# The sample group's HGRN state step moved from the projection into the attention stage, in eight pieces; the page table loaded by one transfer and spread by TensorE

## The chip, the core and the metric

One core of one Trainium2 chip runs the whole program. TensorE (PE) multiplies, VectorE (DVE), ScalarE (ACT) and GpSimd (POOL) do elementwise work, SyncE (SP) issues most transfers and ACT some. Each engine takes its instructions strictly in the order of its own list. The metric is the device time of one execution in microseconds (us).

## The reference, cut to what matters

One decoder layer for two groups of tokens that share weights: a prompt of 1024 tokens and a sample group of 8 sequences with one token each. Half of the heads are sparse attention (compressed, selected and window branches), half are HGRN2, a gated linear recurrence. The projection, in short:

```
z = split(rmsnorm(x, g_pre) @ w_in)      # q_a, k/v of three branches, gates, z_a, q_b, f_b, i_b, z_b
f = lb + (1 - lb) * sigmoid(f_b);  k = (1 - lb) * sigmoid(-f_b);  q = silu(q_b);  v = i_b
```

The prompt runs the recurrence in chunks. For the sample group one step of it is left, and this is what the change moves. For each of 8 sequences and 4 heads, with a state S of 128 x 128 (key by value):

```
S_new = f[:, None] * S + k[:, None] * v[None, :]      # an output, hgrn_state_sample
o     = q @ S_new                                     # then rmsnorm, times silu(z_b)
```

The page table (8 sequences x 8 pages, int32) names the rows of the paged caches that the sample group's attention gathers.

## The kernel before, in words

The program has three stages. **Projection** (`project`): `feat` and `tok` multiply the 1032 normalized tokens with `w_in`; weights and tokens are each split into a high and a low part, so that every product is three fp32r matmuls (`w_hi`, `w_lo`, `xhi`, `xlo`; all matmuls go through the helper at L42, all splits through L50 and L51). `load_w` loads eight tiles `w_raw` per call (three buffers), ACT makes `w_hi` (L238), DVE makes `w_lo` (L239). Between the products stand the prompt's HGRN heads (`hgrn_a`, `hgrn_b`), whose DVE steps `AT` (L490 to L552) sit between PE's `ph` products, and whose last step normalizes `O` on POOL (L608) before PE transposes it (L612). **Attention** (`attention`): units of 128 queries and one key head; each block has two `ph` products, an exponential on ACT (`P`, L955), a mask on POOL (L958 to L962) and four `pb` products. Between the blocks stand the score maxima for the unit after the next: a PE product into `pa` (three banks) that DVE reduces (L909, L916, L918) to `Mp` (L923). Every second block also issues a step of the side work: `sample_attention`, with cache rows gathered into `sg` and turned by PE, then `finish_setup`. **Finish**: output and gate products.

A scheduler with its own timing model sets the order of the instructions on every engine, from the order and priority in the code and from the buffers; an engine's list then runs in order.

`hgrn_sample` (L422 to L467) is a generator that `project` steps through, between the HGRN heads 2 and 3. For each of the four heads it loads the states of all eight sequences (`S`, L437) and v broadcast to 128 partitions (`vb`, L439), 512 KB each. DVE multiplies `vb` by k (L441), POOL multiplies `S` by f (L442), DVE adds (L443), SP stores the new state (L444), ACT and DVE split it into `S0h` and `S0l`, and PE multiplies both parts with a padded q (`qp`), 16 matmuls, whose sums DVE adds to `so` (L452 to L455). Buffers: two for `S` and two for `vb`, shared with tiles of the prompt's heads (tags "S", "O", "F").

`page_index` (L645 to L658) loads the page table by eight transfers of 16 x 8 single elements (L651), so that 16 partitions each hold a sequence's row, and adds a lane number.

Of the kernel before, what the change touches and what calls it, by code (L numbers as in the profile page):

```python
# [20 lines left out]
NB = 8  # L21
# [6 lines left out]
class Kernel:  # L28
# [148 lines left out]
    def load_x(self, ctx):  # L177
# [6 lines left out]
        for i in range(9):  # L184
# [39 lines left out]
    def load_w(self, src, *parts):  # L224

        nc = self.nc
        out = []
        width = sum(p[1] for p in parts)
        for k in range(8):
            raw = self.wpool.tile([128, 512], F32, name="w_raw", bufs=3)[:, :width]  # L230
            o = 0
            for c0, n in parts:
                dma = nc.sync.dma_start(raw[:, o:o + n], src[k * 128:(k + 1) * 128, c0:c0 + n])
                o += n
            hi = self.wpool.tile([128, 512], F32R, name="w_hi", bufs=9)[:, :width]
# [44 lines left out]
    def project(self, ctx):  # L280
        nc, a = self.nc, self.a
# [5 lines left out]
        hp = self.hp = self.pool(hctx, "hg", bufs=2)  # L287
# [15 lines left out]
        K, Q, F = {}, {}, {}  # L303
# [30 lines left out]
        st = [self.hgrn_a(h, Q[h], K[h], F[h]) for h in range(2)]  # L334
        self.tok(C_IB, 512, ev_v)
        self.page_index(self.cp)
        smp = self.hgrn_sample()
        next(smp)
        for h in range(2):
            self.hgrn_b(h, *st[h])  # L340
        self.feat((C_FB + 256, 2, ev_f(2)))
        self.feat((C_QB + 256, 2, ev_q(2)))
        go = lambda n: [next(smp, None) for _ in range(n)]
        for h in range(2, 4):
            st = self.hgrn_a(h, Q[h], K[h], F[h])
            go(2 if h == 3 else 0)
            self.hgrn_b(h, *st)
            go(1 if h == 3 else 0)

        def ev_z(dst, scale):  # L350
            def ev(f, ts, p):
# [35 lines left out]
            nc.scalar.dma_start(self.qh_d[f, :, ts], t.bitcast(F32))  # L387
            nc.scalar.dma_start(self.ql_d[f, :, ts], u.bitcast(F32))

        for _ in smp:  # L390
            pass
        self.aux_rows(hp)
        self.tok(C_KC, 256, ev_kv(0))
        self.tok(C_KS, 256, ev_kv(1))
# [24 lines left out]
                nc.sync.dma_start(self.V[:, br, :, h, :64], self.kv_d[1 + br].rearrange("(i p) c -> p i c", p=128)[:, :, 128 + 64 * h:192 + 64 * h])  # L419
        self.feat((C_ZB, 4, ev_z(self.zb_d, self.hgn)), ps=1)  # L420

    def hgrn_sample(self):  # L422

        nc, hp, a = self.nc, self.hp, self.a
        f, k, q = (self.sfkq[:, i] for i in range(3))
        v_d = self.dram.tile([NB, 512], F32, name="v_d")
        self.after(self.pidma, nc.sync.dma_start(v_d, self.vs))
        o = hp.tile([32, 128], F32, name="so", bufs=1)
        for h in range(4):
            yield  # L430
            po = self.ps_t.tile([128, 512], F32, name="pt")[:64, :128]
            qp = hp.tile([128, NB, 64], F32R, name="qp", bufs=1)
            nc.vector.tensor_scalar(qp.rearrange("p (a c) d -> p a (c d)", c=2), self.ones[:, None, :].to_broadcast([128, 4, 128]), 0.0, None, op0=OP.mult)
            qv = qp.rearrange("p b c -> p (b c)")
            self.split(qv[:, h * NB:h * NB + 456:65], qv[:, 32 + h * NB:32 + h * NB + 456:65], q[:, h], nc.vector, nc.vector)
# [3 lines left out]
            nc.sync.dma_start(vb, bass.AP(tensor=v_d.tensor, offset=v_d.offset + h * 128, ap=[[0, 128], [512, NB], [1, 128]]))  # L439
            bc = lambda t: t[:, h, :, None].to_broadcast([128, NB, 128])  # L440
            nc.vector.tensor_tensor(vb, vb, bc(k), op=OP.mult)  # L441
            nc.gpsimd.tensor_tensor(S, S, bc(f), op=OP.mult)  # L442
            nc.vector.tensor_tensor(S, S, vb, op=OP.add)  # L443
            nc.sync.dma_start(a["hgrn_state_sample"][0, :, h].rearrange("b k v -> k b v"), S)  # L444
            hi = hp.tile([128, NB, 128], F32R, name="S0h", tag="F")
            lo = hp.tile([128, NB, 128], F32R, name="S0l", tag="F")
            self.split(hi, lo, S, nc.scalar, nc.vector)
            for b in range(NB):
                self.mm(po, qp[:, b], hi[:, b], b == 0, False)
                self.mm(po[:32], qp[:, b, :32], lo[:, b], False, b == NB - 1)  # L450
            if h:
                nc.vector.tensor_tensor(o, o, po[:32], op=OP.add)  # L452
            else:
                nc.vector.tensor_copy(o, po[:32])
            nc.vector.tensor_tensor(o, o, po[32:], op=OP.add)  # L455
        sq = hp.tile([32, 128], F32, name="ssq", bufs=1)
        ss = hp.tile([128, 1], F32, name="sr", bufs=1)[:32]
        nc.scalar.activation(sq, o, AF.Square, accum_out=ss)
        nc.vector.tensor_scalar(ss, ss, 1.0 / 128, EPS, op0=OP.mult, op1=OP.add)
        r = hp.tile([128, 1], F32, name="srs", bufs=1)[:32]  # L460
        self.rsqrt(hp, r, ss)
        nc.vector.tensor_scalar(o, o, r, None, op0=OP.mult)
        pt = self.ps_t.tile([128, 512], F32, name="pt")[:, :32]
        nc.tensor.transpose(pt, o, self.ident[:32, :32])
        oT = hp.tile([128, 32], F32, name="soT", bufs=1)
        nc.scalar.copy(oT, pt)
        nc.scalar.dma_start(self.oT_d[:, :, T:].rearrange("h v b -> v h b"), oT.rearrange("p (h b) -> p h b", b=NB))  # L467

# [170 lines left out]

    def side_work(self):  # L640
        with ExitStack() as c:
            yield from self.sample_attention(c)
        yield from self.finish_setup(self.fctx)

    def page_index(self, pool):  # L645

        nc = self.nc
        pt = self.a["page_table"]
        raw = pool.tile([128, NB], I32, name="pt_raw", bufs=1)
        for i in range(8):  # L650
            dma = nc.sync.dma_start(raw[16 * i:16 * i + 16], bass.AP(tensor=pt.tensor, offset=pt.offset + i, ap=[[0, 16], [8, NB]]))  # L651
            if i == 0:
                self.pidma = dma
        lane = pool.tile([128, NB], I32, name="pt_lane", bufs=1)
        nc.gpsimd.iota(lane, pattern=[[0, NB]], base=0, channel_multiplier=1)
        nc.vector.tensor_scalar(lane, lane, 15, None, op0=OP.bitwise_and)
        self.pidx = self.cp.tile([128, NB], I32, name="pidx")
        nc.vector.scalar_tensor_tensor(self.pidx, raw, 16.0, lane, op0=OP.mult, op1=OP.add)  # L658

    def gather(self, out, cache, b):  # L660
        rows = cache[0].rearrange("n (r j) a h d -> (n r) (j a h d)", j=8)
# [733 lines left out]
```

## Time and profile before

| | |
|---|---|
| runs | 1085.47, 1088.88, 1092.77 us; median 1088.88 |
| the profiled execution | 1086.7 us, its span 1085.0 us |
| mean granted clock of TensorE | 0.991 |
| PE busy | 1047.7 us, 97% of the span |
| DVE / ACT / POOL busy | 617.8 / 388.4 / 243.9 us |

The projection's last stores are issued at 546.5 us; attention's exponentials run from 548.1 to 846.4 us, with the finish beside their later part and after it. PE is the engine that is nearly always busy, so what counts is where PE waits, and where its granted clock (1.00 is 2.4 GHz, 0.50 is 1.2 GHz) is low. Idle time of another engine counts only where PE, or the end, waits for it.

### The profile page before, as it was taken

How to read it: one execution, taken by the hardware profiler on the slowest of the kernel's cores; microseconds unless marked ns; L12 is line 12 of the kernel's file. 1: busy time of each engine (PE TensorE's matmuls, PEld its weight loads, DVE VectorE, ACT ScalarE, POOL GpSimd, SP SyncE). 2: the span in 40 equal slices, each digit the busy share in tenths (PEclk: the TensorE clock that was granted, in tenths of full speed). 3: DMA queues.
4: the chain of work that ended last, by engine and by line, in shares of the span. 5: the costliest groups of instructions: out<-in, count | busy, mean ns of one | idle time of the engine just before them, and what ended most of it. 6: DMA issues, size and time to landing. Idle time of an engine off the chain costs nothing.

```text
span 1085.0 us, 18918 instructions
## 1 busy us (share of the span) xinstructions
PE 1047.7 (97%) x7021; PEld 933.6 (86%) x7021; DVE 617.8 (57%) x1822; ACT 388.4 (36%) x786; POOL 243.9 (22%) x276
## 2 busy tenths in 40 slices
PE   4999999999899999999989999999999999999998
PEld 3898799999889899999968888888788888778876
DVE  6847565665494634543665656766665686471223
ACT  4622234313132335432234544553554232241112
POOL 0014232331041133002032211121323133131111
PEclk9999999999989999999989999999999999999999
DMA  6212023323464766403568611001831573121110
GB/s 195 79 29 69 11 72 100 117 89 119 131 176 142 214 210 211 148 1 107 129 215 266 154 29 51 20 21 53 227 106 40 161 209 90 41 97 49 49 35 30
DMA packets 118815, 116.44 MB, mean 107 GB/s; under 512 B 18710, under 2 KB 100974, under 8 KB 116420
## 3 DMA queue, kind: packets, MB, share of 16 engines
q1 hardware_dynamic: 97220, 79.46, 25.7%
q10 hardware_dynamic: 19200, 19.01, 5.1%
q0 software_dynamic: 2304, 16.78, 4.5%
q8 instruction: 55, 0.90, 0.4%
q14 instruction: 36, 0.29, 0.1%
HBM read 84.84 MB, written 29.31 MB: 105 GB/s over the span
## 4 chain that ended last, share of the span: by engine, by line
PE 82%; DMA 9%; DVE 4%; issue 2%; ACT 2%; POOL 1%; SPq 0%; ACTq 0%; DVEq 0%; POOLq 0%
PE pa L42 39%; PE pb L42 26%; PE ph L42 9%; PE pt L42 4%; DMA vb<-v_d 2%; DMA w_raw<-w_in 2%; PE ph L717 1%; PE pa L1125 1%; DMA fw_raw<-w_out 1%; DMA fw_raw<-ple_gate 1%; DMA x_in<-x_prompt 1%; DVE fw_lo L51 1%; PE ph L1319 1%; DMA gpre<-g_pre 0%; DMA f_oa<-oa_d 0%
## 5 line engine op out<-in xcount | busy, mean ns | idle before, releaser
L42 PEld LDWEIGHTS pb<-V,P 128*128 128x128 f32 x1056 | 141.8, 191 | 12.1 <-POOL P L960 1.2
L42 PE MATMUL pb<-V,P 128*128 128x128 f32 x1056 | 148.1, 276 | 0.4 <-DVE mx L909 0.4
L42 PE MATMUL pa<-xhi,w_hi 128*128 128x344 f32 x384 | 126.0, 330 | 2.6 <-ACT w_hi L238 1.1
L42 PE MATMUL pa<-xlo,w_hi 128*128 128x344 f32 x384 | 124.5, 326 | 0.0
L42 PE MATMUL pa<-xhi,w_lo 128*128 128x344 f32 x384 | 123.5, 327 | 0.0
L955 ACT ACTIVATE P<-ph 128x512 f32<-128x512 f32 (+4 forms) x148 | 85.6, 595 | 98.6 <-PE ph L42 69.3
L916 DVE CUSTOM_DVE_ANT_0 junk<-pa,mask 128x320 bf16<-128x320 f32 (+5 forms) x150 | 72.9, 497 | 27.8 <-PE pa L42 26.6
L42 PE MATMUL pa<-w_lo,xhi 128*128 128x256 f32 (+2 forms) x256 | 79.5, 314 | 0.0
L42 PE MATMUL pa<-w_hi,xlo 128*128 128x256 f32 (+2 forms) x256 | 79.2, 314 | 0.0
L42 PE MATMUL pa<-w_hi,xhi 128*128 128x256 f32 (+2 forms) x256 | 78.6, 316 | 0.0
L42 PEld LDWEIGHTS pa<-xhi,w_hi 128*128 128x128 f32 x384 | 73.5, 192 | 4.2 <-ACT w_hi L238 1.7
L238 ACT ACTIVATE w_hi<-w_raw,gpre 128x512 fp32r<-128x512 f32 (+2 forms) x80 | 47.5, 616 | 78.2 <-DMA w_raw<-w_in 43.0
L42 PEld LDWEIGHTS pa<-xlo,w_hi 128*128 128x128 f32 x384 | 73.5, 192 | 0.1
L42 PEld LDWEIGHTS pa<-xhi,w_lo 128*128 128x128 f32 x384 | 73.0, 191 | 0.2
L42 PE MATMUL ph<-QA,KA 128*128 128x512 f32 (+4 forms) x148 | 66.7, 453 | 3.8 <-ACT P L955 2.9
L42 PE MATMUL pa<-KB,QB 65*128 65x320 f32 (+6 forms) x195 | 63.4, 363 | 0.1
L239 DVE SCALAR_TENSOR_TENSOR w_lo<-w_raw,gpre,w_hi 128x512 fp32r<-128x512 f32 (+2 forms) x80 | 50.6, 653 | 21.4 <-ACT w_hi L238 20.7
L42 PE MATMUL pa<-fw_hi,yh 128*128 128x512 f32 (+1 forms) x160 | 61.9, 387 | 0.2 <-ACT fw_hi L50 0.2
L42 PE MATMUL pa<-fw_lo,yh 128*128 128x512 f32 (+1 forms) x160 | 61.6, 385 | 0.0
L42 PE MATMUL pa<-fw_hi,yl 128*128 128x512 f32 (+1 forms) x160 | 61.6, 385 | 0.0
L42 PE MATMUL ph<-QB,KB 68*128 68x512 f32 (+4 forms) x148 | 58.5, 406 | 0.0
L559 POOL TENSOR_TENSOR K<-K,E 128x512 f32<-128x512 f32 x24 | 36.4, 1517 | 94.2 <-PE pb L42 57.2
(457 smaller groups left out, 2411.9 us busy)
## 6 DMA issues: line engine op xcount, KB each, us to landing
w_raw<-w_in SPq DMA_DIRECT2D x32, 256.0 KB
w_raw<-w_in SPq DMA_DIRECT2D x48, 128.0 KB
VS<-sg SPq DMA_DIRECT2D x8, 512.0 KB
sg<-cache_win_kv SPq DMA_DIRECT2D x16, 256.0 KB
fw_raw<-w_out SPq DMA_DIRECT2D x16, 256.0 KB
fw_raw<-ple_gate SPq DMA_DIRECT2D x16, 256.0 KB
f_x<-x_prompt SPq DMA_DIRECT2D x8, 512.0 KB
win_kv_sample<-cache_win_kv SPq DMA_DIRECT2D x8, 511.0 KB
```

Of the source, the lines that this page charges most:

```text
L42: return self.nc.tensor.matmul(out, lhsT, rhs, start=start, stop=stop, skip_group_check=True)
L51: lo_eng.tensor_tensor(lo, src, hi.bitcast(F32), op=OP.subtract)
L238: nc.scalar.activation(hi, raw, AF.Copy, scale=g)
L239: nc.vector.scalar_tensor_tensor(lo, raw, g, hi.bitcast(F32), op0=OP.mult, op1=OP.subtract)
L559: nc.gpsimd.tensor_tensor(Kv[:, :, 0], Kv[:, :, 0], Ev[:, :, 1:2].to_broadcast([128, nb, m]), op=OP.mult)
L717: nc.tensor.transpose(pt[:, i * 128:(i + 1) * 128], src[b0 + j // 2, kv][:, j % 2, 2 * jp:2 * jp + 2].rearrange("p j d -> p (j d)"), self. ...
L916: nc.vector.tensor_tensor_reduce(junk, pm, mk, 1.0, -1e30, op0=OP.add, op1=OP.max, accum_out=o)
L955: nc.scalar.activation(P, ps, AF.Exp, scale=0.125)
L1125: nc.tensor.transpose(pt[:, j * 128:(j + 1) * 128], rows(j), self.ident)
L1319: nc.tensor.transpose(pt[:, c], h[:, k * 128:(k + 1) * 128], self.ident[:n, :n])
```

## The change

The page table comes by one transfer of 8 rows and 8 columns. DVE converts it to float, POOL makes a 0/1 matrix that repeats each row for 16 partitions, and one small matmul spreads it into a PSUM tile, to which DVE adds the lane number. The transfer is ordered behind the last weight transfer of the i_b columns.

The sample group's HGRN step leaves `project`; only the store of v to memory (`v_d`) stays there. `hgrn_sample` now works on half a head at a time (4 sequences, 256 KB per load or store), eight pieces, in a pool of its own with one buffer per tile (`hS`, `hvb`, `hSh`, `hSl`, `qp`), sums in a `pa` bank, and has two yields per piece: after the split, and after the sums. `side_work` steps it from the ninth step of `sample_attention` on, one yield per step. Lines of `attention` and `finish` are 11 higher afterwards.

```diff
@@ load_w
-                dma = nc.sync.dma_start(raw[:, o:o + n], src[k * 128:(k + 1) * 128, c0:c0 + n])
+                dma = self.lastw = nc.sync.dma_start(raw[:, o:o + n], src[k * 128:(k + 1) * 128, c0:c0 + n])
@@ project
         self.page_index(self.cp)
-        smp = self.hgrn_sample()
-        next(smp)
+        self.v_d = self.dram.tile([NB, 512], F32, name="v_d")
+        self.after(nc.sync.dma_start(self.v_d, self.vs), self.pidma)
...
-        go = lambda n: [next(smp, None) for _ in range(n)]
         for h in range(2, 4):
-            st = self.hgrn_a(h, Q[h], K[h], F[h])
-            go(2 if h == 3 else 0)
-            self.hgrn_b(h, *st)
-            go(1 if h == 3 else 0)
+            self.hgrn_b(h, *self.hgrn_a(h, Q[h], K[h], F[h]))
...
-        for _ in smp:
-            pass
         self.aux_rows(hp)
@@ hgrn_sample
+        hp = self.pool(ctx, "hsamp", side="right")
         for h in range(4):
-            yield
-            po = self.ps_t.tile([128, 512], F32, name="pt")[:64, :128]
-            S = hp.tile([128, NB, 128], F32, name="S0", tag="S")
-            vb = hp.tile([128, NB, 128], F32, name="vb", tag="O")
+            for b0 in (0, 4):
+                S = hp.tile([128, 4, 128], F32, name="hS")
+                nc.sync.dma_start(S, a["state_hgrn"][0, b0:b0 + 4, h].rearrange("b k v -> k b v"))
+                vb = hp.tile([128, 4, 128], F32, name="hvb")
+                nc.sync.dma_start(vb, bass.AP(tensor=self.v_d.tensor, offset=self.v_d.offset + b0 * 512 + h * 128, ap=[[0, 128], [512, 4], [1, 128]]))
+                nc.vector.tensor_tensor(vb, vb, bc(k), op=OP.mult)
+                nc.gpsimd.tensor_tensor(S, S, bc(f), op=OP.mult)
+                nc.vector.tensor_tensor(S, S, vb, op=OP.add)
+                nc.sync.dma_start(a["hgrn_state_sample"][0, b0:b0 + 4, h].rearrange("b k v -> k b v"), S)
+                self.split(hi, lo, S, nc.scalar, nc.vector)
+                yield
+                po = self.ps_a.tile([128, 512], F32, name="pa")[:64, :128]
+                for b in range(4):
+                    self.mm(po, qp[:, b], hi[:, b], b == 0, False)
+                    self.mm(po[:32], qp[:, b, :32], lo[:, b], False, b == 3)
...
+                yield
@@ side_work
-            yield from self.sample_attention(c)
+            state = self.hgrn_sample(c)
+            for j, _ in enumerate(self.sample_attention(c)):
+                if j >= 8:
+                    next(state, None)
+                yield
+            for _ in state:
+                yield
@@ page_index
-        for i in range(8):
-            dma = nc.sync.dma_start(raw[16 * i:16 * i + 16], bass.AP(tensor=pt.tensor, offset=pt.offset + i, ap=[[0, 16], [8, NB]]))
+        self.pidma = nc.sync.dma_start(raw, bass.AP(tensor=pt.tensor, offset=pt.offset, ap=[[1, 8], [8, NB]]))
+        self.after(self.pidma, self.lastw)
+        nc.vector.tensor_copy(num, raw)
...
+        self.mm(p, sel, num, True, True)
```

How it moves instructions is shown at three places. The first is SP's list at the start of the projection (L651 and L652 are the page table, L233 weight tiles, L244 copies of a cache):

```order
-L233 DMA w_raw<-w_in 128x256 x6
-L651 DMA pt_raw<-page_table 16x8x1 x7
-L233 DMA w_raw<-w_in 128x256 x10
+L233 DMA w_raw<-w_in 128x256 x16
 L233 DMA w_raw<-w_in 128x512 x8
 L244 DMA win_kv_sample<-cache_win_kv 16x8176 x2
+L652 DMA pt_raw<-page_table 8x8x1
```

The seven transfers that stood between the third and the fourth pair of weight transfers are gone; the single one stands 26 transfers later.

The second is DVE's list in HGRN heads 2 and 3 of the prompt. Before (L441 and L443 are the sample step; AT are the prompt heads' steps for which PE's next `ph` products wait):

```order
L51 TENSOR_TENSOR PRl<-PR,PRh 128x512
L369 COPY z_s<-pa 128x256
L441 TENSOR_TENSOR vb<-vb,sfkq 128x1024
L520 COPY_PREDICATED AT<-lm_496,ph 128x512
L51 TENSOR_TENSOR PQl<-PQ,PQh 128x1024
L490 COPY_PREDICATED AT<-lm_495,pt 128x512
L369 COPY z_s<-pa 128x256 x2
L441 TENSOR_TENSOR vb<-vb,sfkq 128x1024
L513 COPY_PREDICATED AT<-lm_498,ph 128x256x2
```

The same place in the changed program (lines 4 lower here):

```order
L51 TENSOR_TENSOR PRl<-PR,PRh 128x512
L365 COPY z_s<-pa 128x256
L516 COPY_PREDICATED AT<-lm_496,ph 128x512
L51 TENSOR_TENSOR PQl<-PQ,PQh 128x1024
L486 COPY_PREDICATED AT<-lm_495,pt 128x512
L365 COPY z_s<-pa 128x256
L509 COPY_PREDICATED AT<-lm_498,ph 128x256x2
```

The two multiplications of `vb` no longer stand ahead of the steps L520 (now L516) and L513 (now L509).

The third is the attention stage of the changed program. SP's list there (hS and hvb are the pieces' loads, L437 their stores, QA and QB the queries of a later unit):

```order
L437 DMA hgrn_state_sample<-hS 128x4x128
L432 DMA hvb<-v_d 128x4x128
L895 DMA QA<-qh_d 64x4x128
L895 DMA QB_5305<-qh_d 64x4x128
L895 DMA QA<-ql_d 64x4x128
L430 DMA hS<-state_hgrn 128x4x128
L432 DMA hvb<-v_d 128x4x128
L437 DMA hgrn_state_sample<-hS 128x4x128
L430 DMA hS<-state_hgrn 128x4x128
L1006 DMA oa_d<-og 128x256
L432 DMA hvb<-v_d 128x4x128
```

and DVE's list from one piece's multiplication (L434) over its addition (L436) to the next piece's multiplication (L927 and L929 reduce maxima, PT and KT are splits of the sample attention):

```order
L434 TENSOR_TENSOR hvb<-hvb,sfkq 128x512
L51 TENSOR_TENSOR qp<-sfkq,qp 128x4
L927 ISA junk,mx<-pa,mask 128x384
L927 ISA mx 128x1
L920 ISA junk,mx<-pa,mkc 128x64
L920 ISA mx 128x1
L51 TENSOR_TENSOR PT<-pt,PT 128x64x8
L929 TENSOR_REDUCE mx<-pa 128x1
L436 TENSOR_TENSOR hS<-hS,hvb 128x512
L51 TENSOR_TENSOR KT_6932<-pa,KT_6931 128x512
L929 TENSOR_REDUCE mx<-pa 128x1
L434 TENSOR_TENSOR hvb<-hvb,sfkq 128x512
```

On PE the first matmuls of the eight pieces stand at matmul 3609, 3659, 3707, 3740, 3765, 3831, 3892 and 3921 of its list. Every load of a piece stands behind the store of the one before or behind the addition that reads its buffer, and two rows of DVE lie between an addition and the next multiplication, whose load can start only after that addition.

## Rows read from the trace of the kernel before

**Rows 1.** The page, busy time by engine, then the chain that ended last, by line.

```profile
PE 1047.7 (97%) x7021; PEld 933.6 (86%) x7021; DVE 617.8 (57%) x1822; ACT 388.4 (36%) x786; POOL 243.9 (22%) x276
PE pa L42 39%; PE pb L42 26%; PE ph L42 9%; PE pt L42 4%; DMA vb<-v_d 2%; DMA w_raw<-w_in 2%; PE ph L717 1%; PE pa L1125 1%; DMA fw_raw<-w_out 1%; DMA fw_raw<-ple_gate 1%; DMA x_in<-x_prompt 1%; DVE fw_lo L51 1%; PE ph L1319 1%; DMA gpre<-g_pre 0%; DMA f_oa<-oa_d 0%
```

**Rows 2.** Waits of PE: waiting line, what ended it, us in total, times, longest.

```profile
PE ph L42 <- DVE AT L513: 3.6, 1, 3.6
...
PE ph L42 <- DVE AT L520: 2.9, 1, 2.9
...
PE pt L612 <- POOL O L608: 2.6, 1, 2.6
...
PE pa L42 <- ACT w_hi L238: 1.1, 2, 0.9
```

**Rows 3.** The chain that ended last, 280 to 400 us: start, duration, piece of work.

```profile
282.81 5.47 DMA vb<-v_d
288.37 1.23 DVE vb L441
289.60 1.20 DVE AT L520
...
351.77 7.82 DMA vb<-v_d
359.61 1.24 DVE vb L441
361.05 2.86 POOL O L608
...
381.94 0.96 PE pt L42 x16
```

**Rows 4.** Busy time by stretch: engines' busy us, granted clock (PEclk), DMA share, GB/s.

```profile
290.00:300.00 10.00, 6.22 (x44) 5.86 (x44) 5.02 (x7) 0.38 (x2) 0.00 (x0) 0.99 0.57 162
300.00:306.00 6.00, 5.33 (x24) 5.36 (x25) 4.76 (x6) 1.24 (x2) 5.30 (x3) 0.50 0.68 207
364.00:368.00 4.00, 4.00 (x18) 4.00 (x19) 0.05 (x1) 0.68 (x2) 0.00 (x0) 0.59 0.81 265
```

**Rows 5.** The chain and SP's issues in the first 40 us.

```profile
16.85 3.27 SPq L651 DMA_DIRECT2D pt_raw<-page_table  x7
...
20.64 7.24 DMA w_raw<-w_in
...
29.86 2.26 DMA w_raw<-w_in
```

**Rows 6.** Busy time by stretch again: late projection, and attention.

```profile
300.00:320.00 20.00, 19.33 (x198) 18.70 (x199) 18.71 (x36) 7.11 (x12) 10.05 (x6) 0.83 0.55 161
605.00:656.00 51.00, 51.00 (x350) 45.42 (x349) 34.66 (x126) 26.55 (x48) 11.54 (x16) 1.00 0.26 71
```

**Rows 7.** The sample step's operations by line or tile: ns min/median/max, first and last start.

```profile
L442 POOL TENSOR_TENSOR S<-S,sfkq x4: 1898/1900/2495, 300.1 to 354.4; 128x1024 f32<-128x1024 f32 x4
L443 DVE TENSOR_TENSOR S<-S,vb x4: 1203/1218/2155, 302.1 to 360.9; 128x1024 f32<-128x1024 f32 x4
L51 DVE TENSOR_TENSOR S0l<-S,S0h x4: 1206/1209/1226, 308.4 to 378.2; 128x1024 fp32r<-128x1024 f32 x4
L433 DVE TENSOR_SCALAR qp<-ones x4: 404/411/995, 3.1 to 375.9; 128x512 fp32r<-128x512 f32 x4
L455 DVE TENSOR_TENSOR so<-so,pt x4: 278/280/280, 314.4 to 383.2; 32x128 f32<-32x128 f32 x4
```

**Rows 8.** Timeline of POOL and DVE where two of these operations lie beside another engine's.

```profile
302.59 2.50 POOL L442 TENSOR_TENSOR S<-S,sfkq 128x1024 f32<-128x1024 f32 x1 [0.61 <-DMA S<-state_hgrn]
305.05 1.15 POOL L559 TENSOR_TENSOR K<-K,E 128x512 f32<-128x512 f32 x1
...
302.12 1.21 DVE L443 TENSOR_TENSOR S<-S,vb 128x1024 f32<-128x1024 f32 x1
...
305.12 2.15 DVE L443 TENSOR_TENSOR S<-S,vb 128x1024 f32<-128x1024 f32 x1 [1.14 <-POOL S L442]
```

More of the change, by code (lines that the diff above doesn't have):

```diff
@@ L420, in project, with hgrn_sample @@
         self.feat((C_ZB, 4, ev_z(self.zb_d, self.hgn)), ps=1)
-    def hgrn_sample(self):
-        nc, hp, a = self.nc, self.hp, self.a
+    def hgrn_sample(self, ctx):
+        nc, a = self.nc, self.a
         f, k, q = (self.sfkq[:, i] for i in range(3))
-        v_d = self.dram.tile([NB, 512], F32, name="v_d")
-        self.after(self.pidma, nc.sync.dma_start(v_d, self.vs))
-        o = hp.tile([32, 128], F32, name="so", bufs=1)
+        hp = self.pool(ctx, "hsamp", side="right")
+        o = hp.tile([32, 128], F32, name="so")
@@ L429, in hgrn_sample @@
         for h in range(4):
-            yield
-            po = self.ps_t.tile([128, 512], F32, name="pt")[:64, :128]
[L432 to L435, printed above, removed]
@@ L436, in hgrn_sample @@
-            S = hp.tile([128, NB, 128], F32, name="S0", tag="S")
-            nc.sync.dma_start(S, a["state_hgrn"][0, :, h].rearrange("b k v -> k b v"))
-            vb = hp.tile([128, NB, 128], F32, name="vb", tag="O")
[L439 to L457, printed above, removed]
+            for b0 in (0, 4):
+                qp = hp.tile([128, 4, 64], F32R, name="qp")
+                nc.vector.tensor_scalar(qp.rearrange("p (a c) d -> p a (c d)", c=2), self.ones[:, None, :].to_broadcast([128, 2, 128]), 0.0, None, op0=OP.mult)
+                qv = qp.rearrange("p b c -> p (b c)")
+                c0 = h * NB + b0
+                self.split(qv[:, c0:c0 + 196:65], qv[:, 32 + c0:32 + c0 + 196:65], q[:, h, b0:b0 + 4], nc.vector, nc.vector)
+                S = hp.tile([128, 4, 128], F32, name="hS")
+                nc.sync.dma_start(S, a["state_hgrn"][0, b0:b0 + 4, h].rearrange("b k v -> k b v"))
+                vb = hp.tile([128, 4, 128], F32, name="hvb")
+                nc.sync.dma_start(vb, bass.AP(tensor=self.v_d.tensor, offset=self.v_d.offset + b0 * 512 + h * 128, ap=[[0, 128], [512, 4], [1, 128]]))
+                bc = lambda t: t[:, h, b0:b0 + 4, None].to_broadcast([128, 4, 128])
+                nc.vector.tensor_tensor(vb, vb, bc(k), op=OP.mult)
+                nc.gpsimd.tensor_tensor(S, S, bc(f), op=OP.mult)
+                nc.vector.tensor_tensor(S, S, vb, op=OP.add)
+                nc.sync.dma_start(a["hgrn_state_sample"][0, b0:b0 + 4, h].rearrange("b k v -> k b v"), S)
+                hi = hp.tile([128, 4, 128], F32R, name="hSh")
+                lo = hp.tile([128, 4, 128], F32R, name="hSl")
+                self.split(hi, lo, S, nc.scalar, nc.vector)
[4 more added lines that the diff above has]
+                    self.mm(po[:32], qp[:, b, :32], lo[:, b], False, b == 3)
+                if c0:
+                    nc.vector.tensor_tensor(o, o, po[:32], op=OP.add)
+                else:
+                    nc.vector.tensor_copy(o, po[:32])
+                nc.vector.tensor_tensor(o, o, po[32:], op=OP.add)
+                yield
@@ L458, in hgrn_sample @@
+        sq = hp.tile([32, 128], F32, name="ssq")
+        ss = hp.tile([128, 1], F32, name="sr")[:32]
         nc.scalar.activation(sq, o, AF.Square, accum_out=ss)
         nc.vector.tensor_scalar(ss, ss, 1.0 / 128, EPS, op0=OP.mult, op1=OP.add)
-        r = hp.tile([128, 1], F32, name="srs", bufs=1)[:32]
+        r = hp.tile([128, 1], F32, name="srs")[:32]
         self.rsqrt(hp, r, ss)
         nc.vector.tensor_scalar(o, o, r, None, op0=OP.mult)
-        pt = self.ps_t.tile([128, 512], F32, name="pt")[:, :32]
+        pt = self.ps_a.tile([128, 512], F32, name="pa")[:, :32]
@@ L464, in hgrn_sample @@
         nc.tensor.transpose(pt, o, self.ident[:32, :32])
-        oT = hp.tile([128, 32], F32, name="soT", bufs=1)
+        oT = hp.tile([128, 32], F32, name="soT")
         nc.scalar.copy(oT, pt)
@@ L648, in page_index @@
         pt = self.a["page_table"]
-        raw = pool.tile([128, NB], I32, name="pt_raw", bufs=1)
-        for i in range(8):
-            dma = nc.sync.dma_start(raw[16 * i:16 * i + 16], bass.AP(tensor=pt.tensor, offset=pt.offset + i, ap=[[0, 16], [8, NB]]))
-            if i == 0:
-                self.pidma = dma
+        raw = pool.tile([8, NB], I32, name="pt_raw", bufs=1)
+        self.pidma = nc.sync.dma_start(raw, bass.AP(tensor=pt.tensor, offset=pt.offset, ap=[[1, 8], [8, NB]]))
+        self.after(self.pidma, self.lastw)
+        num = pool.tile([8, NB], F32, name="pt_num", bufs=1)
+        nc.vector.tensor_copy(num, raw)
+        sel = self.zpool.tile([128, 688], F32, name="z_s", bufs=2)[:8, :128]
+        nc.gpsimd.memset(sel, 1.0)
+        nc.gpsimd.affine_select(sel, sel, pattern=[[1, 128]], compare_op=OP.is_ge, fill=0.0, base=0, channel_multiplier=-16)
+        nc.gpsimd.affine_select(sel, sel, pattern=[[-1, 128]], compare_op=OP.is_ge, fill=0.0, base=15, channel_multiplier=16)
         lane = pool.tile([128, NB], I32, name="pt_lane", bufs=1)
@@ L656, in page_index @@
         nc.vector.tensor_scalar(lane, lane, 15, None, op0=OP.bitwise_and)
+        lf = pool.tile([128, NB], F32, name="pt_lf", bufs=1)
+        nc.vector.tensor_copy(lf, lane)
+        p = self.ps_t.tile([128, 512], F32, name="pt")[:, :NB]
+        self.mm(p, sel, num, True, True)
         self.pidx = self.cp.tile([128, NB], I32, name="pidx")
-        nc.vector.scalar_tensor_tensor(self.pidx, raw, 16.0, lane, op0=OP.mult, op1=OP.add)
+        nc.vector.scalar_tensor_tensor(self.pidx, p, 16.0, lf, op0=OP.mult, op1=OP.add)
     def gather(self, out, cache, b):
```

## The prediction

> **What bounds the kernel now.** I read four views, from the whole to the place. The page first: PE is busy 97% of the span, and in the chain that ended last nearly every large share is PE's own work; the one transfer of the sample step in it, the load of `vb`, has 2% [rows 1]. So only PE's waits and its clock can give much back. Then PE's waits: three of the longest stand in the projection, 3.6, 2.9 and 2.6 us, on the DVE steps L513 and L520 and on POOL's L608; a wait of 0.9 on `w_hi` belongs to the head [rows 2]. Then the chain through them, read in order of time: the load of `vb` takes 5.47 us, DVE's multiplication of it follows at once (L441, 1.23), and only behind that comes the step L520 that PE waits for. The same at 351.77: 7.82 us of loading, 1.24 on DVE, then POOL's normalization of the prompt's `O`, then PE [rows 3]. DVE stood in its list at a multiplication whose operand was still in flight, with the prompt's work queued behind it. Last the clock by stretch: in 300 to 306 it is 0.50, and in 364 to 368 it is 0.59, each behind one of these waits; in 290 to 300, where two of the waits lie, it is still 0.99 [rows 4].
>
> **What the change takes away.**
> - The three waits. The two multiplications ahead of L520 and L513 are gone from DVE's list, and so is the one ahead of the last head's normalization. Each load that held DVE, 5.47 to 7.82 us, is longer than the PE wait it caused, so I take all of 3.6 + 2.9 + 2.6 = 9.1 us. What is late next there is the prompt's own chain PE, DVE, PE. If the largest wait stayed for that reason, 5.5 us would be left; that is the low end.
> - The clock. Half of the 6 us at 0.50 is lost time, 3.0 us; at 0.59, 41% of 4 us, 1.6 us; 4.6 us in all [rows 4]. With no wait ahead of them both stretches should run at 2.4 GHz. The stretch from 290 to 300 shows that a wait need not be followed by a slow stretch, so the low end is 0 for a wait that stays.
> - The head. SP spends 3.27 us on seven page-table transfers, then the next `w_raw` is 7.24 us under way, where a later one needs 2.26 [rows 5]. ACT's `w_hi` comes late, but PE has other products queued and loses only the 0.9 us [rows 2]. I take 0.9; the bounds are 0 and the 3.27 us of SP.
> - PE's own work is the same 64 matmuls: 16 take 0.96 us [rows 3], 3.8 us in either place.
>
> The gain is 9.1 + 4.6 + 0.9 = 14.6 us.
>
> **What it adds in attention.** In 605 to 656 us, where pieces 3 to 8 will lie, PE is busy all 51 us with 350 matmuls, 0.146 us each, DVE 34.66 us [rows 6]. Two prices are to be compared.
> - DVE's work. At half the size of before, a piece has three long operations of 0.60 us (half of 1203 and 1206 ns), 0.2 for `qp`, two small splits taken at half of a `so` addition, 0.14 each, and two `so` additions of 0.28 [rows 7]: 2.8 us. Six pieces are 17 us: 51.7 of 51. The densest stretch of the projection has DVE at 18.71 of 20 us, 94% [rows 6]; at that share 51.7 needs 55, so PE is held back by about 4 us, less if the maxima lag without harm.
> - The chain of one piece through its single buffers: load, POOL's multiplication, DVE's addition, store, and only then the next load. A load of 128 KB takes 2.26 us [rows 5], one of 512 KB 5.47 [rows 3]; for 256 KB I take 3.3, on the line between them, and the same for the store, which no row shows. SP's two issues are 0.9 (3.27 / 7 each [rows 5]), POOL 0.95 and DVE 0.60 [rows 7]. Together 3.3 + 3.3 + 0.9 + 0.95 + 0.60 = 9.0 us; with both transfers at 2.26 it is 7.0, at 5.47 13.4. Between the first matmuls of pieces 3 and 8 stand 214 PE matmuls, 31 us at 0.146. Five rounds of 9.0 are 45 us; loads may run about one round ahead of PE, so some 5 us are missing. At 7.0 nothing is missing, at 13.4 27 us.
>
> Both prices point at the same place and partly overlap; I take 6 us of PE waits, with 0 and 15 as ends (15 is 45 less 31, no lead at all). The work waiting behind is known: DVE's reductions of maxima stand right behind the multiplication of `hvb` and the addition, PE's next products into `pa` wait for their banks, and on SP the next unit's queries `QA` and `QB` stand behind a store and a load. For the clock I add one slow stretch at the smaller of the two prices, 1.6 us (0 to 4.6). The first piece's `qp` operations come ahead of the first unit's `Mp`: 0.5 us. The small page-table matmul has the time of one in sixteen of 0.96, 0.06 us; its operand is loaded behind the last weights of the v products, and those products, which PE works off first, cover the transfer, so I cost its wait at nothing. If that cover were gone, PE would wait for one small transfer, 2.3 us.
>
> Transfers of 6 MB move from the projection, with its DMA share of 0.57 in 290 to 300 [rows 4], to a stretch with 0.26 [rows 6]; I take no cost for that.
>
> The Trainium skill, page "DMA: Bandwidth & Descriptors", section "Measured (HBM→SBUF, 128 partitions, SWDGE, issued from GpSimd)", speaks against the pieces: it says to batch transfers to 1 MiB or more for three quarters of the peak rate. By its fixed cost of about 2.0 us and 436 GB/s (section "Anatomy of one DMA — SWDGE (gpsimd) path"), an estimate for a piece is 2.6 us per transfer, a chain of 7.7 us and hardly a wait; the trace agrees that there is a fixed part (1.2 us on the line through 2.26 and 5.47 us), but moves the rest at about 120 GB/s [rows 3, 5].
>
> **The sum.** -14.6 + 6 + 1.6 + 0.5 + 0.1 = -6.4. From the profiled execution's 1086.7 that is 1080.3. It lies 2.2 us under the median of the runs, 1088.88, so on that scale 1082.5.
>
> **The rivals.**
> 1. *The cover holds.* Loads run further ahead than one round or the maxima have room, and PE never waits for a piece. For it: PE 100% busy in that stretch with DVE idle a third of it. Against: single buffers, and only 25 matmuls (3.7 us) between pieces 4 and 5. Price: -14.6 + 0.6 = -14.0, on the runs' scale 1074.9.
> 2. *Slower: the chain of single buffers becomes the bound.* From piece 1 to piece 8 stand 312 matmuls, 45.6 us. Seven rounds of 9.0 without lead are 63, which costs 17.4. Each wait of the size of those in the projection [rows 2] may bring a slow stretch; with two, 4.6 more, and DVE held at `hvb` rows holds the maxima for the rest of a load, 3.3 less the two rows between, about 2 us on some two of the pieces, 4 us. In all -14.6 + 0.6 + 17.4 + 4.6 + 4 = +12: 1098.7, on the runs' scale 1100.9. It decides from a round of 6.5 us (45.6 / 7) up, if the loads get no lead. For it: the order of SP's list, where a load stands behind its own buffer's store. Against: the first two pieces have more room.
> 3. *DVE and POOL hold each other up.* An addition beside POOL's L559 took 2.15 us where 1.21 is usual; a POOL multiplication beside a DVE addition took 2.50 where 1.90 is usual [rows 8]. The late one seems to wait for the other's whole operation. POOL is busy 11.5 of 51 us there [rows 6], 30% with 0.95 more for each of four pieces; 24 new long DVE operations, hit three times in ten, at half of the 0.94 us: 3.4 us more waits. Price: -3.0, on the runs' scale 1085.9. The Trainium skill has this as a rule (page "SBUF — State Buffer", section "Who interferes with whom"): a DVE instruction with two SBUF inputs contends with a GpSimd instruction that reads SBUF, and the second fully waits. The trace agrees, with the 0.94 and 0.60 us above.
> 4. *The projection does not give it back.* The prompt's heads wait on their own PE, DVE, PE chain once `vb` is out of the way. Half of the gain, 7.3, against costs of 8.2: +0.9, 1089.8 on the runs' scale. Against: in the chain the loads are the longest pieces by far [rows 3].
>
> **How the numbers follow.** About 1% (10.9 us) is what the runs can tell from no change, since they spread by 7 us. Chances: my forecast 0.32, rival 1 0.27, rival 2 0.16, rival 3 0.14, rival 4 0.11. Faster than 1078 takes rival 1 and a twentieth from the forecast's better end: 0.32. Slower than 1099.8 takes most of rival 2: 0.13. The rest is 0.55. The forecast's own range is 1077 to 1087; the range for 8 in 10 reaches from rival 1's 1074.9 less the head's upper bound (2.4 more), 1072, to 1098, which cuts the upper part of rival 2 and the tails.
>
> **What would show it.** Right: no wait of PE on L516, L509 or L604 (L608 before) above 1 us, the clock at 1.00 in 285 to 370, the first `w_raw` landings without a 7 us one, and between 600 and 670 PE waits of some 6 us in all that end on DVE's reductions or on `hSl`, with DVE waiting for `hvb`. Rival 1 shows attention without such waits; rival 2 shows DVE or POOL waiting for a load in each piece, several us each, and slow stretches; rival 3 shows long `hvb` or `hS` rows on DVE beside POOL's. My forecast is wrong if the waits in the projection stay under other names, or if SP's list delays the queries of a unit.

## The result and the profile after

The change makes the kernel slower: 1101.97 us (median of 6 runs) against 1086.49 us for the kernel before, measured beside it; ratio 1.0121, 95% interval [1.0095, 1.0147]. The forecast was 1082.5 with a range of 1072 to 1098. The profiled execution of the change spans 1098.4 us.

Busy time by stretch, the kernel before. The stretches are the projection up to the first exponential of attention, attention from the first to the last exponential's start, and the rest; columns: stretch, its length, then PE, PEld, DVE, ACT, POOL busy (instructions), granted clock, DMA share, GB/s.

```profile
0.00:548.10 548.10, 520.91 (x3808) 493.46 (x3808) 318.98 (x774) 188.71 (x410) 116.46 (x129) 0.99 0.39 117
548.10:846.40 298.30, 293.06 (x2104) 255.06 (x2105) 188.48 (x782) 140.18 (x250) 74.87 (x116) 0.98 0.37 106
846.40:1085.00 238.60, 233.68 (x1112) 185.03 (x1110) 110.34 (x268) 59.52 (x127) 52.52 (x33) 1.00 0.28 86
```

The same of the changed kernel:

```profile
0.00:530.50 530.50, 511.42 (x3745) 486.49 (x3745) 299.71 (x734) 185.28 (x404) 106.49 (x128) 1.00 0.35 109
530.50:860.00 329.50, 315.23 (x2169) 270.48 (x2170) 216.10 (x860) 146.72 (x261) 82.80 (x124) 0.94 0.41 115
860.00:1098.40 238.40, 233.90 (x1111) 184.92 (x1109) 104.37 (x263) 59.82 (x127) 52.19 (x33) 1.00 0.27 86
```

The balance is in these six rows. The projection is 17.6 us shorter, the rest is unchanged, attention is 31.2 us longer. In attention PE idles 14.3 us (length less PE busy) where it idled 5.2. The mean clock falls from 0.98 to 0.94: the stretches at 0.50 add up to 10.2 us in the attention of before and to 40.9 us in that of the change, and half of such a stretch is lost, 5.1 and 20.5 us. And 64 matmuls more are done there, 3.8 us by their price of before. These three make 28.3 of the 31.2 us.

The projection's gain is where it was expected. The stretch of [rows 3, 4], the kernel before and then the changed one:

```profile
270.00:310.00 40.00, 33.48 (x230) 31.98 (x229) 23.28 (x32) 8.69 (x19) 7.51 (x5) 0.91 0.53 155
```

```profile
270.00:310.00 40.00, 40.00 (x377) 38.66 (x376) 26.13 (x45) 11.10 (x24) 7.37 (x7) 1.00 0.43 130
```

PE has no wait left there and runs at full clock. Waits of PE in the changed kernel (columns as in [rows 2]; left out is the one of 10.4 us at the program's start, the same before):

```profile
PE pa L42 <- DVE mx L927: 4.0, 2, 3.5
PE ph L42 <- ACT P L966: 3.3, 4, 1.7
PE ph L728 <- DVE cr L721: 2.5, 1, 2.5
PE pa L42 <- DVE sm L1072: 2.3, 1, 2.3
PE pa L42 <- DVE Mp L934: 2.3, 3, 1.4
```

The three waits of [rows 2] on L513, L520 and L608 are gone; L728 is a new one of 2.5 us, later in the projection, with a short stretch at half clock behind it; the others are in attention. That stretch:

```profile
370.00:374.00 4.00, 3.02 (x11) 3.02 (x12) 1.79 (x8) 1.85 (x3) 2.25 (x2) 0.59 0.92 324
```

The largest wait of attention, followed through the timelines of DVE and SP (start, duration, instruction, in brackets the idle time ahead and its end):

```profile
611.03 0.69 DVE L436 TENSOR_TENSOR hS<-hS,hvb 128x512 f32<-128x512 f32 x1 [1.30 <-POOL hS L435]
...
618.12 0.69 DVE L434 TENSOR_TENSOR hvb<-hvb,sfkq 128x512 f32<-128x512 f32 x1 [4.37 <-DMA hvb<-v_d]
...
619.13 0.47 DVE L927 CUSTOM_DVE_ANT_0 junk<-pa,mask 128x320 bf16<-128x320 f32 x1
...
624.22 0.69 DVE L436 TENSOR_TENSOR hS<-hS,hvb 128x512 f32<-128x512 f32 x1 [1.69 <-POOL hS L435]
...
628.88 1.39 DVE L434 TENSOR_TENSOR hvb<-hvb,sfkq 128x512 f32<-128x512 f32 x1
```

```profile
611.75 0.38 SPq L437 DMA_DIRECT2D hgrn_state_sample<-hS  x1
612.18 0.50 SPq L432 DMA_DIRECT2D hvb<-v_d  x1
612.77 0.61 SPq L895 DMA_DIRECT2D QA<-qh_d  x1
```

The load of `hvb` could be issued only after the addition at 611.03, stood behind the store, and took 5.84 us in the chain; DVE stood at L434 for 4.37 us with a reduction of maxima behind it, and PE waited 3.5 us for that. What follows costs more (changed kernel, by stretch):

```profile
615.00:620.00 5.00, 1.51 (x12) 1.28 (x11) 1.88 (x6) 0.22 (x1) 1.26 (x1) 0.99 0.40 93
620.00:627.00 7.00, 4.17 (x26) 3.48 (x25) 5.22 (x29) 1.93 (x3) 1.11 (x2) 0.74 0.20 57
627.00:647.00 20.00, 19.57 (x77) 16.23 (x76) 12.48 (x37) 7.29 (x15) 4.09 (x5) 0.50 0.34 101
647.00:660.00 13.00, 13.00 (x95) 11.80 (x95) 8.61 (x30) 4.88 (x9) 4.01 (x5) 0.99 0.25 72
```

For 20 us PE is busy nearly all the time at half clock and does 77 matmuls; the next 13 us hold 95.

### The profile page after: what moved, and what is told of

Same layout as the page of the kernel before. It is cut to its first block, busy times and chain, and to the rows that moved or that the text cites. A ratio compares the mean times of both kernels' runs of the same rounds, so it can differ in the third digit from the quotient of the medians.

```text
span 1098.4 us, 18967 instructions
## 1 busy us (share of the span) xinstructions
PE 1060.6 (97%) x7023; PEld 941.9 (86%) x7023; DVE 620.2 (56%) x1856; ACT 391.8 (36%) x790; POOL 241.5 (22%) x283
## 4 chain that ended last, share of the span: by engine, by line
PE 83%; DMA 6%; DVE 5%; issue 4%; ACT 2%; POOL 0%; SPq 0%; DVEq 0%; POOLq 0%; ACTq 0%
PE pa L42 39%; PE pb L42 26%; PE ph L42 9%; PE pt L42 3%; DMA fw_raw<-w_out 1%; PE ph L728 1%; PE pa L1136 1%; DMA hS<-state_hgrn 1%; DMA hvb<-v_d 1%; DVE junk L927 1%; DMA fw_raw<-ple_gate 1%; DMA cg<-cache_cmp_kv,pidx 1%; DVE fw_lo L51 1%; PE ph L218 1%; DMA w_raw<-w_in 1%
## 5 line engine op out<-in xcount | busy, mean ns | idle before, releaser
L42 PEld LDWEIGHTS pb<-V,P 128*128 128x128 f32 x1056 | 145.4, 198 | 11.3 <-issue 1.1
L42 PE MATMUL pb<-V,P 128*128 128x128 f32 x1056 | 152.6, 284 | 0.6 <-DVE onrm L1000 0.4
L927 DVE CUSTOM_DVE_ANT_0 junk<-pa,mask 128x320 bf16<-128x320 f32 (+5 forms) x150 | 73.4, 496 | 24.1 <-PE pa L42 22.8
L42 PE MATMUL ph<-QA,KA 128*128 128x512 f32 (+4 forms) x148 | 69.2, 470 | 4.3 <-ACT P L966 3.3
L42 PE MATMUL pa<-KB,QB 65*128 65x320 f32 (+6 forms) x195 | 65.8, 369 | 6.7 <-DVE mx L927 4.0
L239 DVE SCALAR_TENSOR_TENSOR w_lo<-w_raw,gpre,w_hi 128x512 fp32r<-128x512 f32 (+2 forms) x80 | 53.1, 684 | 19.6 <-ACT w_hi L238 17.9
L42 PE MATMUL ph<-QB,KB 68*128 68x512 f32 (+4 forms) x148 | 61.0, 423 | 0.0
```

The costliest lines, as they stand in the source:

```text
L42: return self.nc.tensor.matmul(out, lhsT, rhs, start=start, stop=stop, skip_group_check=True)
L927: nc.vector.tensor_tensor_reduce(junk, pm, mk, 1.0, -1e30, op0=OP.add, op1=OP.max, accum_out=o)
```

## Experiments

Theory 1 was what this timeline suggests: engines stand at loads that go through single buffers. Theory 3 holds the transfers and SP's list responsible. Theory 4 is that the pieces' instructions in the engines' lists, in whatever engine, cost attention its time, with the slow clock behind the small gaps of PE. In all, 14 runs; their attention stretch, from the first to the last exponential, by the same view. The time and the ratio are from all executions of a run, the three columns behind them from its one profiled execution:

| run | us | ratio to the kernel before [95%] | attention, us | PE idle in it | clock in it |
|---|---|---|---|---|---|
| kernel before | | 1 | 298.3 | 5.2 | 0.98 |
| the change | 1101.97 | 1.0121 [1.0095, 1.0147] | 329.5 | 14.3 | 0.94 |
| E1 step left out | 1076.36 | 0.9896 [0.9869, 0.9923] | 304.1 | 7.3 | 0.98 |
| E2 no loads | 1096.44 | 1.0087 [1.0057, 1.0117] | 325.9 | 12.2 | 0.94 |
| E3 transfers, split, products | 1088.40 | 1.0007 [0.9986, 1.0027] | 320.7 | 8.7 | 0.94 |
| E4 page table alone | 1082.21 | 0.9938 [0.9913, 0.9962] | 300.0 | 5.6 | 0.98 |
| E5 two buffers | 1098.60 | 1.0097 [1.0067, 1.0126] | 328.7 | 14.9 | 0.95 |
| E6 loads ahead | 1098.04 | 1.0104 [1.0069, 1.0139] | 329.2 | 13.0 | 0.94 |
| E7 no products | 1099.48 | 1.0121 [1.0062, 1.0180] | 322.1 | 14.5 | 0.94 |
| E8 before z_a | 1122.05 | 1.0315 [1.0260, 1.0370] | 294.5 | 3.5 | 0.98 |
| E9 quarter heads | 1127.47 | 1.0351 [1.0290, 1.0413] | 305.7 | 7.2 | 0.97 |
| E10 transfers alone | 1081.39 | 0.9932 [0.9893, 0.9970] | 309.8 | 7.5 | 0.96 |
| E11 on POOL | 1098.22 | 1.0120 [1.0082, 1.0158] | 325.1 | 14.7 | 0.96 |
| E12 late | 1125.75 | 1.0342 [1.0280, 1.0405] | 355.6 | 28.6 | 0.89 |
| E13 own buffers for v | 1075.40 | 0.9860 [0.9827, 0.9894] | 299.8 | 7.1 | 0.98 |
| E14 the change again | 1103.08 | 1.0117 [1.0075, 1.0158] | 334.4 | 15.9 | 0.93 |

**E1.** 

> The change with the sample group's step left out of attention: one memory-to-memory transfer writes the old states as the output, ones stand for its result; everything else as in the change. Theory 1 (attention loses to the pieces, whatever in them): the projection keeps its gain, attention runs as before the change, 17.6 us under the kernel before, ratio about 0.984 (1069 us). Rival (the projection's gain itself upsets attention, by other arrival times and another order of the list): still above 1085.

```diff
-        for h in range(4):
-            for b0 in (0, 4):
...
+        nc.sync.dma_start(a["hgrn_state_sample"][0], a["state_hgrn"][0])
+        nc.vector.tensor_copy(o, self.ones[:32])
+        yield
```

The one transfer is issued at 16.6 us, far ahead of attention. 1076.36: 12 us faster than before, not 17.6. Attention gets most of its length back (304.1), but 6 us stay lost with no piece in it. The list around it is another one: of attention's 2104 matmuls of before, 1972 stand in the same order. The pieces have the other 25 us. That the order costs the 6 us is not shown, but where it is that of before throughout (E4, E13), attention takes 300.0 and 299.8 us.

**E2.** 

> The change with the pieces' two loads left out: DVE and POOL multiply a resident tile of ones by k and f instead of v and the old state, with the same number and size of operations; stores, splits, matmuls stay. Theory 1 (engines stand in their lists for loads that go through single buffers): PE's waits of 3.5 and 2.3 us and the 24 us at half clock go, 1070 to 1077. Rival 2 (the pieces' DVE and POOL work crowds out the maxima, or the two engines hold each other up): as the change, 1095 to 1102.

```diff
-                nc.sync.dma_start(S, a["state_hgrn"]...)
-                nc.sync.dma_start(vb, bass.AP(tensor=self.v_d.tensor, ...))
-                nc.vector.tensor_tensor(vb, vb, bc(k), op=OP.mult)
-                nc.gpsimd.tensor_tensor(S, S, bc(f), op=OP.mult)
+                nc.vector.tensor_tensor(vb, one, bc(k), op=OP.mult)
+                nc.gpsimd.tensor_tensor(S, one, bc(f), op=OP.mult)
```

With nothing to wait for, 1096.44. Attention, by stretch:

```profile
530.50:856.40 325.90, 313.66 (x2168) 268.64 (x2169) 217.45 (x859) 146.71 (x260) 82.16 (x122) 0.94 0.37 103
```

Theory 1 falls: the loads are worth 3.6 of 31.2 us there. The long wait of the timeline was real, and the loads behind it are not the cause of most of the loss.

**E3, E10.** 

> The change with the pieces' arithmetic on the state left out: both loads and the store stay, the store sends the old state as loaded, the split reads a tile of ones; DVE and POOL no longer wait for a load. Theory 1: PE does not wait for a transfer any more, 1068 to 1075. Rival 3 (the transfers themselves, or SP's list with the queries behind them, delay attention): 1090 to 1102.

> The change with only the pieces' loads and stores left in attention (the store sends the old state as loaded, ones stand for the result): no work of DVE, POOL, ACT or PE on a piece. If transfers and SP's list cause the loss (theory 3): about 1088, as with traffic and splits. If the engines' instructions do (theory 4): within 3 us of the run with the step left out, 1074 to 1080.

E3 drops L434, L435 and L436 and splits a tile of ones; E10 drops the split, the products and the sums as well. Attention of E10:

```profile
531.30:841.10 309.80, 302.26 (x2105) 262.67 (x2106) 192.74 (x797) 141.37 (x251) 73.53 (x116) 0.96 0.44 123
```

E10's attention is 5.7 us longer than E1's, nearly all by the clock (PE idles 7.5 us, about as in E1); with split, products and sums (E3) it is 10.9 more (3.8 of them the matmuls themselves), with the state's arithmetic and its waits, the change, 8.8 more. No part holds the loss. These sizes are rough: two profiles of the change itself differ by 4.9 us in attention (E14), and by the ratios of all executions the steps from E1 to E10, E3 and the change are some 4, 8 and 12 us. Nor do the transfers act alone in E10: only 1692 of the 2104 matmuls of before stand in their old order there (1637 in the change), so its part may as well be the order's. E3's 1088.40 lies between its two ranges and decides for neither. E10 confirms theory 4 only in part: it lies 5 us above E1, not within 3.

**E4.** 

> The kernel before with the page-table part of the change alone. The trace of the change is 3.3 us ahead of the kernel before at 44 us. If that gain is kept to the end: ratio 0.997 (3.3 us). As predicted for the head (0.9 us): 0.999. If a later wait swallows it: 1.000.

The edit is the new `page_index` with `lastw` in the old kernel. 0.6% faster (6.1 us by the medians), more than any of the three expectations.

**E5, E6.** 

> The change with two buffers instead of one for the old state and for v of a piece. Theory 1 in its weak form (the chain through single buffers, worth the 5.5 us by which leaving the loads out was faster): 1095 to 1098. Theory 4 (the pieces' instructions in attention's lists, and the slow clock that small gaps of PE bring there, whatever they wait for): 1094 to 1103, with 15 us or more lost to the slow clock. If single buffers were the whole cause, as the prediction's rival 2 has it: 1070 to 1077.

> The change with two buffers, and each piece's loads issued one piece ahead of its arithmetic. Theory 1: DVE and POOL find their operands there, 1092 to 1097. Theory 4: 1094 to 1103.

```diff
-                S = hp.tile([128, 4, 128], F32, name="hS")
-                vb = hp.tile([128, 4, 128], F32, name="hvb")
+                S = hp.tile([128, 4, 128], F32, name="hS", bufs=2)
+                vb = hp.tile([128, 4, 128], F32, name="hvb", bufs=2)
```

Both intervals overlap that of the change. Single buffers as the whole cause are out; between theory 4 and the weak form of theory 1, whose ranges overlap, these two runs can't decide. In E6, which issues the next piece's loads ahead of each piece's arithmetic, PE's largest wait in attention is now for `Mp`:

```profile
PE pa L42 <- DVE Mp L942: 5.6, 3, 3.0
```

PE waits at another place, and its idle time (13.0 us) and the slow clock (0.94) are nearly those of the change.

**E7.** 

> The change with the pieces' 64 matmuls and the additions of their sums left out (ones stand for the result); loads, DVE's, POOL's and ACT's work on the state and stores stay. If the engines' extra work makes PE wait (theory 4a): 3.7 us of PE work less, 1094 to 1098. If the pieces' own short matmuls in PE's list, which wait for the split and hold PE's products behind them, bring the gaps and the slow clock (theory 4b): 1074 to 1082.

It leaves out the loop of `self.mm` and the additions to `o`. 1099.48, with executions from 1091 to 1105 us, and PE idles 14.5 us as in the change: theory 4b falls, 4a stands, though the median lies 1.5 us above its range.

**E11.** 

> The change with the piece's multiplication by k and its addition on POOL, which is 22% busy, instead of DVE; DVE keeps the split and the sums. If DVE's list is what holds PE back: some 12 us of DVE work less, 1086 to 1092 (as with traffic and splits only). If any engine's work does, or POOL holds the masks back: 1098 or more.

```diff
-                nc.vector.tensor_tensor(vb, vb, bc(k), op=OP.mult)
+                nc.gpsimd.tensor_tensor(vb, vb, bc(k), op=OP.mult)
-                nc.vector.tensor_tensor(S, S, vb, op=OP.add)
+                nc.gpsimd.tensor_tensor(S, S, vb, op=OP.add)
```

1098.22: taking this work off DVE does not help; POOL then stands at loads for 15 us (`hvb`) and 11 us (`hS`, 27 us in the change).

**E8, E12, E9.** Three other places for the pieces.

> The pieces, with two buffers and loads one piece ahead, put into the late projection, ahead of the z_a product in the code (the scheduler spreads them among that product's 288 matmuls), sums in a turned-tile bank instead of the attention's; attention as before the change. Theory 4: attention loses nothing against the run with the step left out (1076), plus 3.7 us of matmuls: 1076 to 1082. If the pieces hold up PE anywhere: above 1088.

> The change with the pieces behind the sample attention, one yield in two, instead of among it. If the place among the sample attention's own DVE work is the cause: 1078 to 1088. If attention anywhere loses gaps and clock to the pieces: 1094 to 1104.

> The page-table part of the change, with the sample step left in the projection but in sixteen pieces of two sequences, a pool of its own with two buffers for state and v, loads one piece ahead, the pieces spread from the first HGRN head on; attention as before the change. Theory 4 (what the pieces cost they cost in attention; the projection's loss before was DVE standing at a load): page table -6.1 us, the three projection waits and the clock behind them another -10 to -14: 1066 to 1074. If pieces in the projection hold DVE at their loads again: 1078 to 1090.

In E8 its rival holds; E9 and E12 lie 37 and 22 us outside both of their ranges. E8 calls the generator ahead of `self.feat((C_ZA, ...))`, E12 steps it after `sample_attention`, every second yield, E9 steps it between the HGRN heads. PE, in the order of its list, stood at the pieces' products or at what came behind them; waits of PE in E8, then in E12:

```profile
PE pt L42 <- DVE qp L51: 12.6, 2, 11.3
...
PE pt L471 <- DVE so L469: 6.2, 1, 6.2
```

```profile
PE pa L42 <- ACT hSh L50: 7.1, 3, 4.1
```

In E8 the clock is 0.50 from 533.5 to 598.4 us, with PE busy 37.52 of these 64.9 us. In E9 the loss sits further on, in the compression stage (420 to 460 us: PE busy 14.79 of 40 us, clock 0.62). PE's longest wait there, 11.8 us, is for a load (`pe_t`) that ACT issues at 429.3 us, right behind the store of the sample step's result (L485); what made both so late was not followed up.

**E13, E14.** 

> The page-table part of the change, and the sample step left in the projection as before, but v loaded in halves of 256 KB into three buffers of its own, the first three loads right behind the store of v, long before DVE comes to them; state, splits and products as before; attention untouched. Theory 4 (the loss in the projection was DVE standing at the late load of v; the loss of the change was the pieces in attention): page table -6, waits and clock of the projection -8 to -13: 1068 to 1075. If the waits only move to the load of the state or to POOL: 1080 to 1084, as the page table alone.

> The change itself a second time. If the slow clock in attention belongs to the program: 15 to 23 us of attention at a loss again, 1100 to 1104. If it belongs to the execution: the loss by the clock differs by 5 us or more from 20.5, with the waits of PE in attention again near 14 us.

E13 has the page-table part of the change too (E4), leaves the step where it was and gives v three half-size buffers of its own:

```diff
-            vb = hp.tile([128, NB, 128], F32, name="vb", tag="O")
-            nc.sync.dma_start(vb, ...)
+                vb = vp.tile([128, 4, 128], F32, name="hvb")
+                nc.sync.dma_start(vb, ...)
...
+        for _ in range(3):
+            load_v()
         for h in range(4):
...
+            for b0 in (0, 4):
+                vb, hs = vbs[2 * h + b0 // 4], slice(b0, b0 + 4)
+                nc.vector.tensor_tensor(vb, vb, k[:, h, hs, None].to_broadcast([128, 4, 128]), op=OP.mult)
+                nc.vector.tensor_tensor(S[:, hs], S[:, hs], vb, op=OP.add)
+                load_v()
```

1075.40 us, 1.4% faster than the kernel before and the best version here, 0.4 us above the range of theory 4. Projection and attention, by stretch:

```profile
0.00:536.80 536.80, 516.21 (x3810) 488.54 (x3810) 320.32 (x784) 188.72 (x410) 112.89 (x132) 1.00 0.39 120
536.80:836.60 299.80, 292.72 (x2104) 255.05 (x2105) 188.88 (x782) 140.08 (x250) 75.22 (x116) 0.98 0.38 106
```

The projection is 11.3 us shorter with all its matmuls in it (6.0 of them in E4, by the page table alone), and attention about as before. The change again (E14) loses in attention what it lost the first time, and a little more:

```profile
530.30:864.70 334.40, 318.49 (x2168) 272.24 (x2169) 215.98 (x860) 146.44 (x261) 81.44 (x124) 0.93 0.40 114
```

The slow clock belongs to the program: a lower mean in the same stretch both times.

## Why the prediction was wrong, step by step

- **The waits and the clock of the projection**: right in mechanism, and in the sum partly by luck. With the head, 14.6 us of gain and 3.8 us of matmuls leaving the stage were forecast, 18.4; 17.6 was measured. The three waits and the two slow stretches are gone, but a new wait of 2.5 us at L728 and the slow stretch behind it, 1.6 us, take part of that back, and the head, which gave 3.3 us where 0.9 were forecast, fills most of the gap. **Rival 4** is out.
- **The head**: mis-sized, too small. Forecast 0.9, the upper bound being 3.27. The kernel before, then the changed one, whose PE hardly idles any more from 22 to 40 us:

```profile
20.00:28.00 8.00, 6.92 (x26) 6.32 (x26) 3.64 (x19) 1.99 (x5) 0.00 (x0) 1.00 0.26 75
28.00:40.00 12.00, 10.62 (x67) 9.80 (x68) 10.71 (x42) 10.15 (x18) 1.44 (x1) 1.00 0.53 149
```

```profile
20.00:28.00 8.00, 7.52 (x34) 7.27 (x35) 7.19 (x29) 5.56 (x9) 0.00 (x0) 1.00 0.67 176
28.00:40.00 12.00, 12.00 (x83) 11.95 (x82) 10.47 (x46) 9.62 (x19) 2.48 (x3) 1.00 0.29 81
```

  The trace is 3.3 us ahead there (the expectation of E4 has it from the change's trace), and alone (E4) the edit gives 0.62%, 6.7 us. The wait on `w_hi` alone was not what the late `w_raw` cost. In E4's trace the projection is 6.0 us shorter: the same matmuls come 4.4 us earlier at 61 us, and most of the rest is gained at the HGRN heads, where two of the three waits of [rows 2] are shorter, 2.1 and 1.8 us for 2.6 and 2.9:

```profile
PE pt L612 <- POOL O L608: 2.1, 1, 2.1
...
PE ph L42 <- DVE AT L520: 1.8, 1, 1.8
```

- **PE's waits in attention**, "I take 6 us": 9.1 more than before, inside the bounds of 0 and 15. The wait that was described is there, 3.5 us behind the multiplication of `hvb`. But the working behind the size failed, and that the size came near is luck. It let DVE be filled to 94%; in 600 to 660 us DVE was busy 39.06 of 60, against 37.38 before, while PE got through 309 matmuls there instead of 420: DVE was never full. And it mixed two ways of counting: the 214 and 312 matmuls are counted in the program's list, but the 0.146 us are those of a row of the trace, which has two rows for each `pb` product of attention (1056 rows `pb<-V,P` for 528 products). The trace of the change has 281 and 416 rows between the same places, which is 41 and 61 us at that price, not 31 and 46. Five rounds of 9.0 us are then 4 us more than the cover, not 14 (the prediction has 15 for 45 less 31; and its 27 us for rounds of 13.4 are 22 by its own rule). The loads of the chain between 593 and 623 us took 2.7 to 5.8 us, where 3.3 was taken. The rounds through single buffers are there, and longer than forecast (9.4 to 14.1 us between the last six additions; 13.2 from the one at 611.03 to the next at 624.22), yet without loads (E2) or with two buffers (E5, E6) the loss is nearly the same.
- **The clock**, "one slow stretch at the smaller of the two prices, 1.6 us (0 to 4.6)": this is the step that made the forecast wrong. The clock cost 15.4 us more than before (20.5 less 5.1), more than three times the upper end. I priced a slow stretch by the two short ones of [rows 4]; in attention one lasted 20 us with PE busy nearly throughout. A long one stood in the trace of before as well, at the start of attention, and was not used as a price; the change has one of the same length in the second row:

```profile
549.00:559.00 10.00, 8.35 (x29) 6.19 (x29) 8.83 (x35) 4.61 (x8) 3.01 (x10) 0.50 1.03 363
```

```profile
530.00:545.00 15.00, 12.85 (x52) 9.02 (x51) 11.74 (x43) 5.54 (x10) 5.33 (x13) 0.66 1.01 331
```

- **Rival 2** has the sign and nearly the time (1100.9) by another mechanism: seven rounds without lead, 17.4 us of waits. By the trace's own count of matmuls these are some 2 us, and the runs refute it as the whole cause (E2, E5, E6): that it came near is luck. **Rival 1** is out. **Rival 3** is seen in two of the pieces' 24 long operations on DVE, 1.0 us in all where 3.4 were priced: in DVE's timeline above, the multiplication at 628.88 took 1.39 us, where the one at 618.12 took 0.69; POOL's L1001 runs beside it. That row agrees with the rule cited there from the Trainium skill (page "SBUF — State Buffer", section "Who interferes with whom").

What the runs show in place of the forecast: the pieces in attention cost 25 of the 31.2 us (E1), and no single layer of them holds that loss. By the profiles, from 298.3 us: without any piece 5.8 (E1), with transfers 5.7 more (E10), with split, products and sums 10.9 more (E3), with the arithmetic on the state and its waits 8.8 more; each of these is uncertain by some 5 us. Half of the sum is the slow clock. What stays open is why the clock stays low so long while PE is busy, and how much of each layer is the scheduler's other order; no run with pieces in attention kept the order fixed.

## What to carry to other kernels

A stage in which PE is 98% busy and its fillers are idle a third of the time is not free room: here attention lost 31 us, of which new waits are 9 and the lower clock 15. Where one engine stands at a late operand, give that operand its own buffers and load it earlier before moving its work elsewhere (E13: 13.5 us by the medians of its runs, of which the page table alone gave 6.1 in E4). And take one suspected cause away at a time before believing a timeline: without the loads behind the longest wait, attention got back 3.6 of its 31.2 us (E2). When a list's instructions are priced by rows of a trace, check first that both count the same thing.

## What was not expected of the hardware

The granted clock was 0.50 for 20 us in which PE was busy 19.57 us. It also fell with no wait of PE that the trace shows: in E1, after 16 matmuls of 16 x 8 that took 1.95 us, PE being busy in every one of these stretches.

```profile
730.00:733.80 3.80, 3.80 (x31) 3.52 (x30) 0.48 (x3) 0.95 (x2) 0.63 (x1) 0.99 0.01 2
733.80:737.20 3.40, 3.40 (x14) 3.01 (x13) 1.50 (x5) 0.60 (x1) 0.13 (x1) 0.51 0.00 0
737.20:740.00 2.80, 2.80 (x19) 2.09 (x18) 2.19 (x15) 1.73 (x3) 0.00 (x0) 1.00 0.00 0
```

The Trainium skill (page "TensorE: Matmul & The Clock Gate", section "What's actually happening") puts the penalty of the ramp, the slow start, under 1% of a typical kernel's span. What is lost here is not at the start of the kernel but in stretches from 299 us on: the kernel before, with a mean clock of 0.991, stays under 1%; the change, at 0.979, loses 2.1%.
